# A hybrid encoder layer on one core: x's squares regrouped behind the projection of p, and the side work's steps with every twelve matmuls

## The chip, the cores and the metric

The kernel runs on one core of a Trainium2 chip. The metric is the device time of one execution in microseconds (us); lower is better. The engines are named as in the profile: PE is the matrix engine and PEld its weight loads, DVE the vector engine, ACT the scalar engine, POOL the general engine, and SP the engine whose queue issues nearly all DMAs here (SPq).

## The reference, cut to what matters

Two sequences (512 and 256 tokens) pass through one layer with the same weights. All 768 tokens are worked on together. Cut to what the change touches:

```
hn   = x * rsqrt(mean(x*x) + eps) * norm_g          # 768 x 2048
proj = hn @ w_in                                    # split into s_x, s_z, q, k, v, a_z, g_s, g_a
y    = s5(s_x, ssm parameters)                      # a state-space branch, two directions
...
h    = h + sigmoid(rmsnorm(h) @ ple_gate_w) * (p @ ple_proj_w)
```

`p @ ple_proj_w` doesn't depend on anything else, so the kernel does it first, while x is loaded. The sum of squares over the 2048 features gives one scale a token, and the kernel applies it to the results of the matmuls rather than to x.

## The kernel before, in words

x is held with features on the partitions: 16 tiles of 128 features by 768 tokens, loaded as eight pairs (`x_load`, 768 KB each, six buffers `xr`). Matmuls run on a high and a low half of each operand (ACT makes the high half, DVE the rest: `hh`/`hl` for x, in the trace tile `a`; `wh`/`wl` for weights), three products for each pair of halves.

The order of all work is written out by hand. `blocks` lists the matmul work; `run_blocks` walks it in groups of twelve matmuls. Around each group it calls `slot_e` (before) and `slot_p` (after). These let the side work go one step further: generators in a queue (`lane`), each of which has a part for ACT and DVE (E, before the group) and a part for PE (P, behind it). `pace[0]` is how far a group moves the step's counter: at 0.5 two groups share a step, at 0.7 ten groups have seven steps, at 1.0 each group has its own. `later(fn, n)` runs `fn` n steps on. Each engine works its instructions in the order of this program.

The stretch in question:

- Four `Proj` blocks, 16 groups, pace 0.5, so eight steps. Each group ends one 128 x 768 tile of `p @ ple_proj_w` in two banks of PSUM; ACT copies one half into a `stg` buffer, DVE the other (line 573), and a store (`d_pp`) follows one step later. There are five `stg` buffers and eight banks. With it runs the first part of the generator `x_gen`: step s makes the halves of x tiles 2s and 2s+1.
- Then eight s_x blocks (`Feat`), 64 groups, eight groups a block and four a weight piece. At the start of each piece `ahead` splits the piece after the next one (`wh`, `wl`, three buffers each). `x_gen` goes on: the rest of the squares (ACT, `sq`, three buffers) are added into `sqa` (DVE), two tiles a step; then `token_scale` sums `sqa` over partitions on PE (`ssps`), takes the root on POOL, and turns it into rows on PE (`rps`) for the tile `R`. No s_x result can leave PSUM before `R`; the first block's end is put off by five steps for that.
- Behind `x_gen` in the same queue stand the state-space steps: `s5_params` (bias matmuls `bb`, then small DVE operations on tiles `p_...`, and eight ACT copies into `tw` and `tq`), and then `s5_half(0)`, which waits until the fourth s_x block has left. Its first PE work is a transpose `wps` of DVE's product `w`. It sets its own pace (0.9, later 0.82 and 1.0).

After the regrouped part nothing else in the program is edited: `s5_half` starts by the block's end, not by the pace.

Of the kernel before, what the change touches and what calls it, by code (L numbers as in the profile page):

```python
# [28 lines left out]
class Lane:  # L29
# [5 lines left out]
    def add(self, gen):  # L35
        self.q.append(gen)
# [12 lines left out]
def build(tc, d, dbg=None):  # L49
    nc = tc.nc  # L50
    es = ExitStack()
    with es:
        es.enter_context(tc.manual_schedule())
        _build(tc, nc, d, es, dbg)


def _build(tc, nc, d, es, dbg):
# [20 lines left out]
    def act(out, in_, func=AF.Copy, **kw):  # L78
        return nc.scalar.activation(out=out, in_=in_, func=func, **kw)  # L79

    def tt(out, a, b, op):
        return nc.vector.tensor_tensor(out=out, in0=a, in1=b, op=op)  # L82
# [6 lines left out]
    def stt(out, a, s, b, op0, op1):  # L89
        return nc.vector.scalar_tensor_tensor(out=out, in0=a, scalar=s, in1=b, op0=op0, op1=op1)  # L90
# [7 lines left out]
    def dma(out, in_):  # L98
        return nc.sync.dma_start(out=out, in_=in_)  # L99
# [15 lines left out]
    pace = [0.5]  # L115
# [375 lines left out]
    def token_scale(acc, rs, rest=0):  # L491

        for _ in range(2 * rest):
            yield
        yield
        sp = bank(6, "ssps")
        for t in range(NT):
            mm(sp[:, 2 * t:2 * t + 2], acc[:, t * 128:(t + 1) * 128], ones[:, 0:2], True, True)
        yield
        rsqrt_mean(rs, sp[:, 0:2 * NT].rearrange("p (t x) -> p t x", x=2)[:, :, 0], D)  # L500
        rb = stg()
        for t in range(NT):
            ts(rb[:, t * 128:(t + 1) * 128], ones, rs[:, t:t + 1])
        yield
        rp = [bank(4, "rps"), bank(5, "rps")]
        for t in range(NT):
            nc.tensor.transpose(rp[t // 3][:, t % 3 * 128:t % 3 * 128 + 128], rb[:, t * 128:(t + 1) * 128], ident)
        yield
        act(R[:, :HT], rp[0][:, :HT])
        nc.vector.tensor_copy(out=R[:, HT:], in_=rp[1][:, :HT])  # L510
        yield
        yield
# [11 lines left out]
    def x_load(i):  # L524
        if i < 8:
            xraw[i] = ax.tile([128, 2, T], F32, tag="xr", name="xr", bufs=6)
            dma(xraw[i], d["xT"][:, 2 * i:2 * i + 2])

    def x_gen():

        sqs = []
        acc = ax.tile([128, T], F32, name="sqa")

        def square(k):
            sq = ax.tile([128, T], F32, tag="sq", name="sq", bufs=3)
            act(sq, xraw[k // 2][:, k % 2], AF.Square)
            sqs.append((k, sq))

        def add():
            while sqs:  # L540
                k, sq = sqs.pop(0)
                if k:
                    tt(acc, acc, sq, A_)
                else:
                    nc.vector.tensor_copy(out=acc, in_=sq)

        for s in range(8):
            add()
            for i in range(2):
                k = 2 * s + i  # L550
                x = xraw[s][:, i]
                act(hh[k], x, AF.Copy, scale=norm_g[:, k:k + 1])
                stt(hl[k], x, norm_g[:, k:k + 1], hh[k].bitcast(F32), M, S_)
            if 1 <= s < 5:
                square(s - 1)
            if s in (0, 3, 5):
                x_load({0: 5, 3: 6, 5: 7}[s])
            yield
            yield
        for s in range(4, 16, 2):  # L560
            add()
            square(s)
            square(s + 1)
            yield
            yield
        add()
        yield from token_scale(acc, rs_x)
        ax_es.close()
# [691 lines left out]
    def lam_gen():  # L1260

        pr = sm.tile([128, 2], F32, tag="lam", name="lampr")
        tt(pr, lamv[:, 0:2], lamv[:, 2:4], M)
        ts(subg8, subg, 0.8)
        yield
        lp = bank(7, "lamps")
        mm(lp[:, 0:2], ones, pr, True, True)
        yield
        e = sm.tile([128, 2], F32, tag="lam", name="lame")
        act(e, lp[:, 0:2], AF.Exp)  # L1270
        tt(nlam, e[:, 1:2], e[:, 0:1], S_)
        ts(nlam, nlam, -(0.8 - 0.6), None, A_)
        yield
        yield
# [604 lines left out]
    def run_blocks(lo, hi):  # L1879

        j = start_of[lo]
        while j < start_of[hi]:
            blk, pi = pieces[j]
            if isinstance(blk, Quad):
                run_quad(blk, j)
                j += 2
                continue
            if pi == 0:
                if blk.pre:
                    blk.pre()  # L1890
                blk.begin()
            ahead(j)
            wh, wl = halves.pop(j)
            for sub in range(4):
                prod[0] += 1
                hook(j, sub)
                run_events()
                if quad_of(j + 1):
                    for st in (("x",), ("a22",), ("s2",), ("y",))[sub]:
                        pieces[j + 1][0].step(st, j + 1)  # L1900
                    if sub == 3:
                        more()
                slot_e()
                blk.mms(pi, sub, wh, wl)
                slot_p()
            if blk in early:
                ahead(j + 1)
            if pi == len(blk.pieces) - 1:
                if blk.wait:
                    later(blk.end, blk.wait)  # L1910
                else:
                    blk.end()
                if blk.post:
                    blk.post()
            j += 1
# [52 lines left out]
    for i in range(2, 5):  # L1968
        x_load(i)
    wsplit(1)  # L1970
    lane.add(x_gen())
    lane.add(s5_all())
    run_blocks(0, end_p)
    j = start_of[first_k0]
    hooks[j, 0] = [lambda: lane2.add(t_prep(0))]
    lane.add(lam_gen())
    pace[0] = 0.7
    run_blocks(end_p, end_p + 4)
    run_blocks(end_p + 4, first_k0)
    while "s5" not in done:  # L1980
# [140 lines left out]
```

## Time and profile before

| what | value |
|---|---|
| median of three runs | 2394.75 us (2393.71 to 2396.52) |
| the profiled execution's own time | 2396.96 us |
| its span, first to last instruction | 2395.2 us |
| mean granted TensorE clock | 0.996 |

The span leaves out 1.8 us of the profiled execution's time. Busy times of the engines overlap each other. Idle time of an engine matters only where the engine that sets the end is the one idle.

### The profile page before, as it was taken

How to read it: one execution, taken by the hardware profiler on the slowest of the kernel's cores; microseconds unless marked ns; L12 is line 12 of the kernel's file. 1: busy time of each engine (PE TensorE's matmuls, PEld its weight loads, DVE VectorE, ACT ScalarE, POOL GpSimd, SP SyncE). 2: the span in 40 equal slices, each digit the busy share in tenths (PEclk: the TensorE clock that was granted, in tenths of full speed). 3: DMA queues.
4: the chain of work that ended last, by engine and by line, in shares of the span. 5: the costliest groups of instructions: out<-in, count | busy, mean ns of one | idle time of the engine just before them, and what ended most of it. 6: DMA issues, size and time to landing. Idle time of an engine off the chain costs nothing.

```text
span 2395.2 us, 36700 instructions
## 1 busy us (share of the span) xinstructions
PE 2352.4 (98%) x14278; PEld 2316.1 (97%) x14278; DVE 1442.2 (60%) x2689; ACT 1042.1 (44%) x1845; POOL 131.4 (5%) x158
## 2 busy tenths in 40 slices
PE   8999999999999999999999999999999999999997
PEld 8899999999999999999999999899999999999986
DVE  7577673566726677655667675556466655554346
ACT  7243214342135555554555555653233443533233
POOL 0000000000000000000121111000000011100000
PEclk9999999999999999999999999999999999999999
DMA  8344245432465677675867777456336485922235
GB/s 322 105 112 119 89 127 160 131 118 95 128 187 160 203 228 204 180 220 152 198 132 163 167 152 197 141 190 211 133 133 204 119 204 117 256 82 89 82 110 178
DMA packets 158157, 377.09 MB, mean 157 GB/s; under 512 B 34912, under 2 KB 57824, under 8 KB 157984
## 3 DMA queue, kind: packets, MB, share of 16 engines
q1 hardware_dynamic: 139264, 324.15, 41.4%
q0 software_dynamic: 18144, 49.55, 12.9%
q8 instruction: 112, 1.84, 0.3%
q10 hardware_dynamic: 576, 1.05, 0.1%
q14 instruction: 61, 0.50, 0.1%
HBM read 250.75 MB, written 129.43 MB: 159 GB/s over the span
## 4 chain that ended last, share of the span: by engine, by line
PE 86%; DMA 4%; DVE 4%; issue 3%; ACT 2%; SPq 1%; POOL 0%; POOLq 0%; ACTq 0%; DVEq 0%
PE acc L93 78%; PE yps L93 2%; PE o L93 1%; PE vps L93 1%; PE kps L93 1%; PE s L93 1%; DVE a L82 1%; DVE wl L82 1%; ACT wh L79 1%; DMA d_ga<-stg 1%; PE wps L1054 1%; SPq L99 1%; DMA xr<-in_xT 1%; DMA a<-in_xT 1%; ACT a L79 1%
## 5 line engine op out<-in xcount | busy, mean ns | idle before, releaser
L93 PE MATMUL acc<-a,wh 128*128 128x384 f32 (+2 forms) x5976 | 1331.1, 335 | 4.3 <-ACT stg L79 3.0
L93 PEld LDWEIGHTS acc<-a,wh 128*128 128x128 f32 x5976 | 1060.8, 188 | 12.7 <-ACT stg L79 3.9
L93 PE MATMUL acc<-a,wl 128*128 128x384 f32 (+2 forms) x3360 | 886.9, 337 | 6.6 <-DVE wl L82 3.7
L93 PEld LDWEIGHTS acc<-a,wl 128*128 128x128 f32 x3360 | 605.0, 188 | 16.5 <-DVE wl L82 4.1
L82 DVE TENSOR_TENSOR wl<-raw,wh 128x1024 fp32r<-128x1024 f32 (+1 forms) x280 | 340.7, 1217 | 425.5 <-ACT wh L79 420.3
L79 ACT ACTIVATE wh<-raw 128x1024 fp32r<-128x1024 f32 (+2 forms) x332 | 326.0, 983 | 297.3 <-PE acc L93 259.3
L79 ACT ACTIVATE stg<-acc 128x384 f32<-128x384 f32 x396 | 189.5, 489 | 382.1 <-PE acc L93 334.4
L93 PE MATMUL acc<-y,wh 128*128 128x384 f32 (+2 forms) x920 | 201.3, 335 | 0.0
L93 PEld LDWEIGHTS acc<-y,wh 128*128 128x128 f32 x920 | 162.7, 188 | 0.9
L93 PE MATMUL acc<-wh,a 128*128 128x256 f32 x768 | 138.8, 283 | 0.0
L79 ACT ACTIVATE stg<-stg 128x768 f32<-128x768 f32 (+3 forms) x64 | 43.3, 686 | 179.9 <-DVE stg L82 179.9
L93 PEld LDWEIGHTS acc<-wh,a 128*128 128x128 f32 x768 | 119.7, 192 | 0.0
L93 PE MATMUL acc<-y,wl 128*128 128x384 f32 (+2 forms) x400 | 109.8, 335 | 1.6 <-DVE wl L82 1.6
L93 PE MATMUL acc<-wl,a 128*128 128x256 f32 x384 | 109.8, 286 | 0.0
L93 PE MATMUL acc<-a,wa 128*128 128x384 f32 x504 | 94.8, 336 | 2.1 <-ACT stg L79 2.1
L93 PEld LDWEIGHTS acc<-a,wa 128*128 128x128 f32 x504 | 87.6, 188 | 2.9 <-ACT stg L79 2.8
L93 PEld LDWEIGHTS acc<-y,wl 128*128 128x128 f32 x400 | 72.9, 188 | 2.3 <-DVE wl L82 1.8
L82 DVE TENSOR_TENSOR raw<-raw,raw 128x512 f32<-128x512 f32 x104 | 71.9, 691 | 3.0
L93 PEld LDWEIGHTS acc<-wl,a 128*128 128x128 f32 x384 | 73.6, 192 | 0.0
L82 DVE TENSOR_TENSOR raw<-raw 128x512 f32<-128x512 f32 x104 | 71.6, 689 | 1.8
L82 DVE TENSOR_TENSOR stg<-stg,acc 128x384 f32<-128x384 f32 x52 | 28.8, 554 | 66.5 <-PE acc L93 52.6
L82 DVE TENSOR_TENSOR stg<-acc,R 128x384 f32<-128x384 f32 (+2 forms) x48 | 29.3, 656 | 63.4 <-PE acc L93 63.4
(251 smaller groups left out, 2319.0 us busy)
## 6 DMA issues: line engine op xcount, KB each, us to landing
raw<-in_w_in SPq DMA_DIRECT2D x144, 512.0 KB, 4.3
raw<-in_ple_g_w SPq DMA_DIRECT2D x42, 512.0 KB, 3.6
raw<-in_w_out SPq DMA_DIRECT2D x32, 512.0 KB, 4.1
d_h<-stg POOLq DMA_DIRECT2D x34, 384.0 KB, 6.6
d_gs<-stg POOLq DMA_DIRECT2D x28, 384.0 KB, 6.2
d_ga<-stg POOLq DMA_DIRECT2D x28, 384.0 KB, 5.9
d_q<-q SPq DMA_DIRECT2D x16, 512.0 KB, 3.7
raw<-in_w_v SPq DMA_DIRECT2D x16, 512.0 KB, 4.3
```

The lines of the kernel that those rows point to most:

```text
L79: return nc.scalar.activation(out=out, in_=in_, func=func, **kw)
L82: return nc.vector.tensor_tensor(out=out, in0=a, in1=b, op=op)
L93: return nc.tensor.matmul(out, lhsT, rhs, start=start, stop=stop, **kw)
L99: return nc.sync.dma_start(out=out, in_=in_)
L1054: nc.tensor.transpose(wps[x][:, g * 128:(g + 1) * 128], w[:, x, g], ident)
```

## The change

In the first eight steps, before: step s begins with the adds of the squares made earlier, then makes the halves of two tiles, and steps 1 to 4 make one square each (tiles 0 to 3). After: steps 1 and 3 make two squares each (tiles 0, 1 and 2, 3), behind the halves; steps 2 and 4 add them, two at a time, also behind the halves; the adds at the front of each step are gone. The loads of x pairs 6 and 7 go with steps 2 and 4 instead of 3 and 5. As many tiles as before (12) are squared in the s_x blocks. The pace in the s_x blocks until `s5_half` sets its own is 1.0 instead of 0.7.

```
-            add()
             for i in range(2):
                 ...
-            if 1 <= s < 5:
-                square(s - 1)
-            if s in (0, 3, 5):
-                x_load({0: 5, 3: 6, 5: 7}[s])
+            if s == 0:
+                x_load(5)
+            elif s in (1, 3):
+                for k in range(2):
+                    square(s - 1 + k)
+            elif s in (2, 4):
+                add()
+                x_load(s // 2 + 5)
             yield
             yield
...
     lane.add(lam_gen())
-    pace[0] = 0.7
+    pace[0] = 1.0
     run_blocks(end_p, end_p + 4)
```

## Rows read from the trace of the kernel before

**Rows 1.** The page: busy us of each engine, share of the span, instructions.

```profile
PE 2352.4 (98%) x14278; PEld 2316.1 (97%) x14278; DVE 1442.2 (60%) x2689; ACT 1042.1 (44%) x1845; POOL 131.4 (5%) x158
```

**Rows 2.** Waits of PE, first 160 us: us in total, times, longest.

```profile
PE wps L1054 <- DVE w L82: 3.0, 2, 1.6
...
PE ssps L93 <- DVE sqa L82: 0.2, 1, 0.2
```

**Rows 3.** Timeline of PE, 25 to 48 us: start, us, instruction [idle before].

```profile
34.81 0.33 PE L93 MATMUL acc<-ph,wh 128*128 128x384 f32 x1
36.10 0.44 PE L93 MATMUL acc<-ph,wh 128*128 128x384 f32 x1 [0.96 <-DVE stg L573]
...
44.41 0.51 PE L93 MATMUL acc<-a,wl 128*128 128x384 f32 x2
```

**Rows 4.** Timeline of ACT, from 29 us on.

```profile
29.64 1.00 ACT L79 ACTIVATE stg<-acc 128x384 f32<-128x384 f32 x2
30.54 1.05 ACT L79 ACTIVATE wh<-raw 128x1024 fp32r<-128x1024 f32 x1
...
44.07 1.77 ACT L79 ACTIVATE a<-xr,consts 128x768 fp32r<-128x768 f32 x2 [2.21 <-DMA xr<-in_xT]
...
47.76 3.12 ACT L79 ACTIVATE sq<-xr 128x768 f32<-128x768 f32 x4
...
126.82 2.28 ACT L79 ACTIVATE tw<-p_pw 64x512 f32<-64x512 f32 x2 [11.39 <-DVE p_pw L82]
...
135.91 1.06 ACT L79 ACTIVATE wh<-raw 128x1024 fp32r<-128x1024 f32 x1
```

**Rows 5.** Timeline of DVE, from 31 us on.

```profile
31.62 1.23 DVE L82 TENSOR_TENSOR wl<-raw,wh 128x1024 fp32r<-128x1024 f32 x1 [0.53 <-ACT wh L79]
32.77 0.95 DVE L82 TENSOR_TENSOR sqa<-sqa,sq 128x768 f32<-128x768 f32 x1
33.63 1.94 DVE L90 SCALAR_TENSOR_TENSOR a<-xr,consts,a 128x768 fp32r<-128x768 f32 x2
35.49 1.01 DVE L573 COPY stg<-acc 128x384 f32<-128x384 f32 x2
...
49.04 4.14 DVE L82 TENSOR_TENSOR sqa<-sqa,sq 128x768 f32<-128x768 f32 x4
54.02 1.23 DVE L82 TENSOR_TENSOR wl<-raw,wh 128x1024 fp32r<-128x1024 f32 x1 [0.84 <-ACT wh L79]
...
97.83 0.19 DVE L87 TENSOR_SCALAR p_xcp_dt<-p_ldt 128x64 f32<-128x64 f32 x1
...
127.67 0.19 DVE L861 COPY a8i<-p_pw 128x64 f32<-128x64 f32 x1
...
141.84 1.23 DVE L82 TENSOR_TENSOR wl<-raw,wh 128x1024 fp32r<-128x1024 f32 x1 [1.80 <-ACT wh L79]
...
146.36 0.69 DVE L82 TENSOR_TENSOR w<-t,t 128x512 f32<-128x512 f32 x1
```

**Rows 6.** Groups of DVE by line, 44 to 68 us: busy, mean ns, idle before.

```profile
L82 DVE TENSOR_TENSOR sqa<-sqa,sq 128x768 f32<-128x768 f32 x12 | 11.5, 957 | 0.8
```

**Rows 7.** DMA issues, 27.8 to 28.2 us: KB each, median us to landing.

```profile
xr<-in_xT SPq DMA_DIRECT2D x1, 768.0 KB, 7.8
```

**Rows 8.** The chain that ended last, first 160 us: start, us, what.

```profile
67.61 1.50 PE ssps L93 x12
...
72.48 8.34 PE acc L93 x48
```

**Rows 9.** Windows: stretch, length, busy of PE, PEld, DVE, ACT, POOL, PEclk, DMA.

```profile
140.00:150.00 10.00, 7.00 (x42) 6.45 (x42) 8.07 (x14) 2.63 (x4) 0.00 (x0) 1.00 0.33 120
```

**Rows 10.** Windows around the first fall of the clock, same columns.

```profile
409.00:412.00 3.00, 0.94 (x7) 0.81 (x7) 1.85 (x3) 1.06 (x1) 0.00 (x0) 0.94 0.98 268
412.00:415.00 3.00, 3.00 (x16) 3.00 (x16) 0.62 (x3) 0.00 (x0) 0.00 (x0) 0.50 0.59 176
```

**Rows 11.** Timeline of PE at that fall.

```profile
411.47 1.86 PE L93 MATMUL yps<-sb,q 128*128 128x96 f32 x8 [2.06 <-DVE wl L82]
```

## The prediction, as it was put on record before the run

> **What bounds the kernel now.** I read the page's busy times first: PE is busy 2352.4 of 2395.2 us [rows 1], so the whole idle time of PE is 43 us, and an edit off PE counts only by the PE idle it opens or closes. Next the waits of PE in the first 160 us, which is all that the edits reach: the reader sees 3.0 us in two waits of the transposes `wps` for DVE's `w` and 0.2 us of `ssps` for the sum of squares [rows 2]; the other waits there are the start and three short ones in the projection. Then the timelines of PE, ACT and DVE side by side. In the projection PE once waits 0.96 us for a DVE copy out of PSUM [rows 3]; from there to 142 us it runs without a gap, but for that 0.2. So the stretch holds little to win (about 3 us at 142 to 147 us, 1 us at 35), and DVE's order decides both. A group of twelve matmuls takes 8.34 / 4 = 2.085 us [rows 8].
>
> **The change part by part.**
>
> *What doesn't move.* I counted the pace's steps by hand. Before, the twelve late squares take groups 0 to 8 of the s_x blocks, `ssps` stands behind group 10, `R` at 12, the parameters' end at 33. After, the squares take groups 0 to 5, `ssps` stands behind group 6, `R` at 8, `tw`/`tq` at 20 (before 29), the parameters' end at 23. But `s5_half(0)` waits for the fourth block in both: its first step is at group 33 in both, its scan at 87, its output at 126, the end of the second half at 255. From group 126 on the two orders are almost the same. So no gain or loss is expected there; only the first 45 groups count. The 12 + 4 squares and adds are the same instructions.
>
> *Squares in the projection, two a step.* In step 3 ACT makes one more square ahead of the copies at 29.64 and of the weight half at 30.54 [rows 4]. A square in a row of four costs 3.12 / 4 = 0.78 us [rows 4]. So the weight half goes back by that, and DVE's `wl`, which waits for it, from 31.62 to 32.4 [rows 5]. On DVE the old order is `wl`, one add (0.86 to the next start), two x halves (1.86), then the copies at 35.49 [rows 5], the first of which lets PE go on at 36.10 [rows 3]. The new order is `wl` (1.15 to the next start), two halves (1.86), two adds, then the copies. Two adds into one `sqa` cost 1.06 + 0.86: four in a row take 4.14 with 0.957 for one [rows 5, 6], hence (4.14 - 0.96) / 3 = 1.06 from start to start. 32.4 + 1.15 + 1.86 + 1.92 = 37.3 for the copies, and PE went on 0.61 after their start (36.10 - 35.49), so now at 37.9: **+1.8 us**. Its gap there grows from 0.96 to between 2.4 and 2.8 us (its work before ends at 34.81 + 0.33, and comes some 0.3 later as its own copy waits for the extra square). Below, the bound is 0 (if the adds found room behind `wl`); above, 2.6 (no overlap at all). I take 1.8, all of its terms being rows.
>
> *The x loads.* Pair 6 is issued some 8 us sooner, ahead of two stores of p. A load issued at 27.87 landed 7.8 us later [rows 7]; ahead of the stores it can hold back theirs by up to 3 us, and with them the `stg` buffers four groups on. ACT reaches those after the landing, so I take 0; 1 us at the most. Pair 7 lands before its 2.21 us wait on ACT at 44.07 [rows 4]. That wait is off PE's path, but it lets ACT and DVE take up the 1.8 us: the first late square still starts near 47.6 (before 47.76 [rows 4]), the first add near 48.9 (before 49.04 [rows 5]), as PE begins s_x at 44.41 + 1.8 = 46.2 [rows 3].
>
> *Pace 1.0 in s_x: the sum of squares.* Twelve adds at 1.06 are 12.7 us, and one weight split (1.15) stands among them, with some 0.85 us of DVE idle before it, as before (0.84 at 54.02 [rows 5]). The ACT half queues behind a square that waits for a buffer, which an add must free. 48.9 + 14.7 = 63.6. PE comes to `ssps` after seven groups: 46.2 + 14.6 = 60.8. So PE now waits **2.85 us** for DVE, with all later s_x groups queued behind. Before, four more groups (8.3 us) covered this; this is the cover that the pace takes away. Less the old 0.2 us [rows 2]: with the projection, +4.5 us. If DVE starts an add or two sooner or later, this moves by 1 us either way.
>
> [...] With 0.957 for each the twelve adds would be 1.2 us shorter and the total that much lower.
>
> *The parameters, earlier.* On DVE they run from 97.83 to 127.86 [rows 5], and ACT copies `tw` and `tq` from 126.82 to 135.91 [rows 4]. They push back the weight half at 135.91, `wl`, then `wl` at 141.84 and `w` at 146.36 [rows 5], for which PE waits 3.0 us [rows 2]. After, PE comes to group 12 at 80.7 us (63.6, the 1.50 of `ssps` [rows 8], six groups, and about 3 us of other small matmuls). There DVE has a weight split and the first block's evacuation, some 3.8 us; from 84.5 the parameters follow without a gap. Between 97.83 and 127.86 they shared DVE with two splits and one evacuation, about 4 us, so they are 26 us; with two evacuations and two splits among them they end near 115, and the copies, 9.1 us, near 124. The split due at group 32 (126.3 us by the same count) stands behind the copies on ACT and comes at 126.4: it nearly fits. `w` is done near 144.9, its transposes are due at 145.1. I take **-2.7 us**, bounds 0 (if the `s5_half` loads come 3 us later) and -3.0.
>
> *The clock.* [...] At 140 to 150 us PE stood idle 3.0 us in all, in pieces of at most 1.6 [rows 2], and the clock stayed at 1.00 [rows 9]. The change opens gaps of about 2.4 and 2.85 us; each is longer than the gap with a fall. I take one fall; bounds none and two.
>
> *Sum.* +1.8 + 2.85 - 0.2 - 2.7 + 1.7 = **+3.5 us**. Against the profiled execution (2396.96 us, which is 2.2 above the median) that is 2400.5; against the median of the runs, 2394.75 + 3.5 = **2398.3 us**, +0.15%. A change of 0.2% is 4.8 us, about what a measurement of this kernel can tell from none.
>
> **The rivals.**
>
> *Slower: the clock falls behind both gaps.* Its place is 38 and 64 us. For it: both gaps are longer than the 2.06 us one. Against: only one gap of this size is in the rows I use, and the lengths are my working. It decides if what followed the gap at 409 us follows here twice. +1.8 (the sum without a fall) + 3.4 = +5.2 us, 2400.0; with the projection's 1 us for the stores, 2401. Chance 0.28.
>
> *The adds cost less, or DVE starts sooner.* With 0.957 us for an add, or without the 0.85 us in front of the split, the second gap is 1.7 to 2.0 us, and it may leave the clock alone. For it: a lone add lasts 0.957 [rows 6]. Against: the row of four at 4.14 [rows 5]. +1.8 - 1.2 = +0.6 up to +2.3 with one fall: 2395.4 to 2397. Chance 0.26. Here too belongs that the change does next to nothing on PE: if both its gaps and the old one at 142 us net out.
>
> *Faster: the old stall at 409 us goes with its fall.* The shift of the steps by a group in the half before it could bring the operand in time: -2.06 - 1.7 us, and -2.7 at 142 us, if the new gaps stay under 1 us. That is -5.5 us, 2389.3. Against: the steps stand at the same groups from 126 on, and the adds alone are 12.7 us for 14.6 us of groups, with a start 2.7 us late. Chance 0.06.
>
> **How the numbers follow.** The forecast with one fall has 0.40, and gives 2397.3 to 2399.4 by the bounds of its terms. Faster 0.06 (the last rival), slower 0.28 (the first), same 0.66. The range runs from the cheaper adds, 2395.4, less 1 us for DVE's start and 1 us for the spread of the runs, 2393.5, to both falls, 2400, with 2.5 us for the stores and for the split that nearly fits, 2402.5; outside lie most of the last rival and the tail of the others.
>
> **What the profile after would show.** PE waits for `ssps` some 2.85 us near 61 to 64 us (below 1 us: the add chain is wrong). The wait for the copy near 35 to 38 us is over 2 us (unchanged: the order on DVE was misread). The granted clock shows a new piece at the lower level near 38 or 64 us. The `wps` wait near 145 us is under 0.5 us; `tw` and `tq` are done by 125 us. From 150 us on everything is the old trace, moved by one amount. The prediction fails if a wait appears that I did not find, above all PE at group 32 for its weight split, which has 0.1 us to spare by my working, or if the later stalls move.

## The result, and the profile after

The changed kernel takes 2412.38 us (median of four runs, 2408.68 to 2414.26) against 2395.64 us for the kernel before, run beside it: ratio 1.0063, 95% interval 1.0048 to 1.0077. The forecast was 2398.3 us, +0.15%, and the range ended at 2402.5: wrong, by some 14 us. The profiled execution took 2412.77 us, its span is 2411.0 us.

The page first, busy times (answers to [rows 1]). PE's busy time grows by 6 us of the 16; the rest is idle time of PE.

```profile
span 2411.0 us, 36698 instructions
PE 2358.6 (98%) x14278; PEld 2323.9 (96%) x14278; DVE 1444.0 (60%) x2689; ACT 1040.6 (43%) x1845; POOL 130.8 (5%) x158
```

**The first 160 us.** The waits of PE (answers to [rows 2]; us in total, times, longest) and PE's timeline (start, us, instruction, [idle before]; answers to [rows 3, 8]):

```profile
PE ssps L93 <- DVE sqa L82: 2.4, 1, 2.4
PE acc L93 <- DVE stg L577: 2.2, 1, 2.2
```

```profile
34.77 0.34 PE L93 MATMUL acc<-ph,wh 128*128 128x384 f32 x1
37.28 0.44 PE L93 MATMUL acc<-ph,wh 128*128 128x384 f32 x1 [2.17 <-DVE stg L577]
...
47.15 0.51 PE L93 MATMUL acc<-a,wl 128*128 128x384 f32 x2
...
64.30 2.14 PE L93 MATMUL ssps<-ones,sqa 128*128 128x2 f32 x12 [2.43 <-DVE sqa L82]
...
148.92 1.03 PE L1058 MATMUL wps<-consts,w 128*128 128x128 f32 x8
```

Both gaps that the prediction announced are there: 2.17 us for the copy out of PSUM (before 0.96) and 2.43 us for the sum of squares (before 0.2). The transposes `wps` run in one piece, without a wait. DVE's timeline shows why (answers to [rows 5, 6]):

```profile
31.81 1.23 DVE L82 TENSOR_TENSOR wl<-raw,wh 128x1024 fp32r<-128x1024 f32 x1 [1.12 <-ACT wh L79]
...
34.81 1.95 DVE L82 TENSOR_TENSOR sqa<-sqa,sq 128x768 f32<-128x768 f32 x2
36.68 1.01 DVE L577 COPY stg<-acc 128x384 f32<-128x384 f32 x2
...
49.84 6.27 DVE L82 TENSOR_TENSOR sqa<-sqa,sq 128x768 f32<-128x768 f32 x6
...
58.05 6.20 DVE L82 TENSOR_TENSOR sqa<-sqa,sq 128x768 f32<-128x768 f32 x6
...
138.32 0.23 DVE L82 TENSOR_TENSOR u<-kr,bc 128x64 f32<-128x64 f32 x1 [4.73 <-DMA bc<-in_bc]
...
145.91 0.69 DVE L82 TENSOR_TENSOR w<-t,t 128x512 f32<-128x512 f32 x1
```

The copy starts at 36.68 behind the two adds; the twelve adds end at 64.25 (58.05 + 6.20). The second `w` starts at 145.91, almost as before (146.36 [rows 5]). PE doesn't wait for it because PE itself is late. The windows show the clock (length, then busy of PE, PEld, DVE, ACT, POOL, then PEclk and DMA; answers to [rows 9, 10]):

```profile
36.00:40.00 4.00, 2.72 (x9) 2.72 (x10) 4.00 (x7) 3.30 (x5) 0.00 (x0) 0.71 0.90 353
...
65.00:68.00 3.00, 3.00 (x13) 3.00 (x13) 0.16 (x1) 0.00 (x0) 1.21 (x1) 0.50 0.00 0
...
140.00:150.00 10.00, 10.00 (x63) 9.96 (x62) 8.21 (x13) 2.40 (x3) 0.00 (x0) 1.00 0.30 99
409.00:412.00 3.00, 3.00 (x24) 3.00 (x24) 0.00 (x0) 1.51 (x4) 0.00 (x0) 1.00 0.39 77
412.00:415.00 3.00, 3.00 (x20) 3.00 (x19) 0.00 (x0) 0.88 (x4) 0.00 (x0) 1.00 0.86 249
```

The clock falls to 0.50 behind both gaps (in each us from 38 to 41, with 0.71 in the mean of 36 to 40; and in each from 65 to 71), and the stall near 411 us with its fall [rows 10, 11] isn't there.

**Where the 16 us are.** PE does the same 12,624 matmuls into `acc` in the same order in every kernel here. So I set each against the same one of the kernel before. The table gives how many us later it starts, at times of the kernel before, worked out from the traces of one profiled execution each. How far two executions scatter is seen from the line of e11: on every engine it runs the same instructions in the same order as the kernel before, and the two lie up to 3.6 us apart. So a difference of 2 or 3 us between two lines shows nothing by itself. (e1 to e12 are the experiments below.)

```
us            44   125   165   405   418  1250  1320  1470  1600  2380
after        2.7   7.7   3.8   5.9   2.0   4.0  12.7  19.2  15.8  16.0
e1           3.4   6.7   2.8   6.3   2.4   4.5   7.2   6.8   6.4   6.4
e2          -0.3  -0.3  -0.3  -0.3  -4.2  -1.7   6.9  13.3  10.2  10.3
e8           0.2   0.2   0.2   0.2  -3.7  -0.5   7.5   9.1   6.3   6.2
e11          0.1   0.1   2.5   2.5  -1.4   1.4   2.6   2.5   3.6   2.9
e3           1.6   1.6   2.7   2.7   0.0   1.5   2.3   4.1   4.5   4.7
e4           0.0   6.5   2.6   4.6   0.7   1.3   1.0   1.1   2.6   1.8
e7           1.4   6.4   6.4   8.1   6.8   4.5   4.2   4.4   5.1   5.2
e5           1.1   4.4   0.5   4.0   0.1   2.8   4.8   9.3   5.8   6.0
e6           0.0   0.1   2.4   2.4  -1.2   0.0  -1.0  -0.7   0.4  -0.1
e9           0.1   5.6   1.7   5.2   1.3   2.2   2.6   2.6   2.7   2.9
e10         -0.4   5.0   1.2   4.7   2.5   2.3   2.2   2.4   1.8   1.9
e12         -0.3  -0.2  -0.2  -0.2  -3.6  -3.0  -1.7  -3.1  -0.4  -0.9
```

The first line answers the question of place: at 165 us the changed kernel is 3.8 us late, close to the forecast of 3.5. Then it stays between 2 and 6 us late until 1250 us. From there to 1600 us it loses another 11.8 us: in the attention, more than a millisecond behind the last edited line. The waits of PE in that stretch, 1060 to 1600 us of each kernel, before and after:

```profile
PE acc L93 <- ACT stg L79: 5.1, 5, 1.6
...
PE wt L1387 <- DVE p L90: 4.1, 1, 4.1
```

```profile
PE acc L93 <- ACT stg L79: 14.5, 8, 4.8
PE s L93 <- ACT ot L79: 3.1, 3, 1.2
```

The wait for ACT's copy out of PSUM goes from 5.1 to 14.5 us, and one for `ot` is new. The longest, 4.83 us, is followed through three engines in the changed kernel's timelines of DVE, ACT and PE:

```profile
1280.57 1.82 DVE L82 TENSOR_TENSOR kl<-raw,kh 128x768 fp32r<-128x768 f32 x2
...
1285.61 0.69 DVE L82 TENSOR_TENSOR wh<-raw,wh 128x512 fp32r<-128x512 f32 x1 [0.27 <-ACT wh L79]
1288.38 0.96 DVE L90 SCALAR_TENSOR_TENSOR raw<-raw,R 128x768 f32<-128x768 f32 x1 [2.07 <-DMA raw<-d_qq]
1291.43 0.96 DVE L90 SCALAR_TENSOR_TENSOR raw<-raw,R 128x768 f32<-128x768 f32 x1 [2.09 <-DMA raw<-d_qq]
1292.31 0.69 DVE L82 TENSOR_TENSOR raw<-raw 128x512 f32<-128x512 f32 x1
```

```profile
1293.09 0.63 ACT L79 ACTIVATE wl<-raw 128x512 fp32r<-128x512 f32 x1 [5.94 <-DVE raw L82]
1293.62 1.56 ACT L79 ACTIVATE qh<-raw 128x768 fp32r<-128x768 f32 x2
1295.09 0.47 ACT L79 ACTIVATE stg<-acc 128x384 f32<-128x384 f32 x1
```

```profile
1295.61 2.61 PE L93 MATMUL acc<-a,wh 128*128 128x384 f32 x7 [4.83 <-ACT stg L79]
```

Read it from the bottom. PE needs a PSUM bank that ACT empties at 1295.09. Ahead of that copy ACT has a weight's half `wl`, which waits 5.94 us for DVE's `raw` at 1292.31. Ahead of that DVE has the scaling of q, which waits twice for the reload of q from `d_qq`. That reload goes into the buffer that k has just left (`kl`, done at 1282.39), so it is issued then, from 1282.45 us on, and DVE starts on its halves 5.9 and 9.0 us later. Before, the scaling of q costs a 1.32 us wait on DVE, 2.64 on ACT and 0.68 on PE. It also stands at another place in DVE's order: ahead of the weight's `wh`, where the changed kernel has it behind (1285.61 above). DVE's rows of the kernel before, then PE's:

```profile
1280.72 1.87 DVE L90 SCALAR_TENSOR_TENSOR raw<-raw,R 128x768 f32<-128x768 f32 x2 [1.32 <-DMA raw<-d_qq]
1282.50 0.68 DVE L82 TENSOR_TENSOR wh<-raw,wh 128x512 fp32r<-128x512 f32 x1
```

```profile
1284.94 2.35 PE L93 MATMUL acc<-a,wh 128*128 128x384 f32 x12 [0.68 <-ACT stg L79]
```

What put the steps of the attention elsewhere? A counter: `slot_p` adds the pace behind each group and closes the step when the sum reaches 1 (the next `slot_e` opens a new one); what is left over stays. After the state-space steps both kernels stand at group 256, as I had counted, but the rest left in the counter (`open_[1]`) is 0.16 before and 0.56 after. By the count of the program the two part where the state-space steps set their own pace: 35 groups at 0.7 leave a rest of 0.50, 34 at 1.0 leave none, and the stages behind carry this on.

The paces that follow group 256 are the same in both, so the rest lives on. At pace 0.5 (715 to 993 us in the kernel before) two groups share a step, and it depends on the rest, below or above a half, which two. The attention enters the queue at 993 us: with 0.16 in the middle of an open step, with 0.56 at the start of one. By the count of the program this, with 24 groups at 0.9, puts its parts half a step later, so that they change places with what the program writes between two groups: halves of weights and copies out of PSUM. Where the loss arises, from 1250 us on, the pace is 1.0 (until 1506 us) and each group has its own step in both kernels; what differs there is the order on DVE and ACT.

### The profile page after: what moved, and what is told of

Its sections match the earlier page's. It is cut to its first block, busy times and chain, and to the rows that moved or that the text cites. A ratio compares the mean times of both kernels' runs of the same rounds, so it can differ in the third digit from the quotient of the medians.

```text
span 2411.0 us, 36698 instructions
## 1 busy us (share of the span) xinstructions
PE 2358.6 (98%) x14278; PEld 2323.9 (96%) x14278; DVE 1444.0 (60%) x2689; ACT 1040.6 (43%) x1845; POOL 130.8 (5%) x158
## 4 chain that ended last, share of the span: by engine, by line
PE 85%; DMA 5%; DVE 4%; ACT 3%; issue 2%; SPq 1%; POOL 0%; POOLq 0%; ACTq 0%; DVEq 0%
PE acc L93 78%; PE yps L93 1%; PE vps L93 1%; PE kps L93 1%; PE o L93 1%; SPq L99 1%; PE s L93 1%; DVE a L82 1%; ACT wh L79 1%; ACT a L79 1%; DMA raw<-d_qq 1%; DMA d_o<-ot 1%; ACT stg L79 1%; PE wps L1058 1%; DMA stg<-d_y 1%
```

## The experiments

All ratios are against the kernel before, run beside each on the same chip, with 95% intervals. My theory: the counter's rest makes the loss in the attention. The rival: some resource state, a queue or a lateness that the change carries along, makes it.

**The counter alone, both ways.** e1 is the changed kernel with the old rest; e2 is the kernel before with the new rest, and nothing of the change.

```
     while "s5" not in done:
         slot_e()
         slot_p()
+    open_[1] = 0.1599999999999877      # e1; in e2 0.5599999999999894
```

e1: 

> The changed kernel, but where the state-space steps are done (group 256) the fraction left in the pace's counter is set to 0.16, which is what the kernel before has there; the changed one has 0.56. Nothing else differs. Theory of the counter: from group 256 on each step falls on the same group as before again, so the loss in the attention (lag 5.9 us at 1084 us, 18 at 1450) goes, and only the first 150 us cost: the lag there was 3 to 4 us, so 2396 + 3.5 = 2399 us, 2397 to 2402. Rival, the shift: the attention loses because it runs 4 us later against its transfers, or by some other state carried on; then this stays near 2412.

Measured: 1.0014 (1.0005 to 1.0024), 2400.91 us.

e2: 

> The kernel before with the counter set to 0.56 at group 256, nothing else changed. Theory of the counter: the whole loss of the attention appears without any part of the change, 2396 + 12 = 2408 us (2405 to 2412), with the two long waits near 1290 and 1385 us. Rival, the shift: nothing moves before group 256, so 2396 us.

Measured: 1.0045 (1.0029 to 1.0060), 2409.07 us. The table has the same in its stretches: from 1250 to 1600 us e1 loses 1.9 us, e2 11.9, the changed kernel 11.8. And e2's rows of DVE and PE repeat those of the changed kernel:

```profile
1282.18 0.96 DVE L90 SCALAR_TENSOR_TENSOR raw<-raw,R 128x768 f32<-128x768 f32 x1 [2.11 <-DMA raw<-d_qq]
1285.30 0.96 DVE L90 SCALAR_TENSOR_TENSOR raw<-raw,R 128x768 f32<-128x768 f32 x1 [2.16 <-DMA raw<-d_qq]
```

```profile
1289.48 4.21 PE L93 MATMUL acc<-a,wh 128*128 128x384 f32 x12 [4.93 <-ACT stg L79]
```

So the loss there is the counter's, shown from both sides. The rival falls: e1 comes 4.5 us late to the attention and loses little, e2 comes 1.7 us early and loses all.

**Other rests.** The kernel before with 0.86 (e8) and 0.36 (e11) in the same line.

e8: 

> The kernel before with the counter at 0.86 at group 256. Theory of the counter says that the phase matters, not which way it goes: I expect a loss of a few us, 2396 to 2408, or none, and the waits of the attention at other places than with 0.16 or 0.56. Rival (the loss comes from 0.56 being later than 0.16 by two fifths of a step, so more of it costs more): 2412 us or more.

Measured: 1.0039 (1.0025 to 1.0052). The loss is of the size that I expected, but not by waits at other places: PE's long wait near 1285 us is that of e2 (4.97 us, in e2 4.93), and the second one, near 1385 us, is missing in this execution.

e11: 

> The kernel before with the counter's rest set to 0.36 instead of 0.16 at the end of the state-space steps, halfway to the 0.56 that the change leaves. My theory (what counts is which group of the seven products the reload of q and its scaling fall in, a step function of the rest): either nothing (1.000) or most of the loss (1.003 to 1.005), and the waits for the ACT copy at 1283 to 1296 us show which. Rival (the loss grows evenly with the rest): about half of 0.56's, 1.002.

Measured: 1.0006 (0.9997 to 1.0015). The traces show why. Every engine of e11 runs the instructions of the kernel before in the same order, from the first to the last; and e8 has e2's order but for one place near 1070 us on DVE and on ACT. So the four rests give two orders, not four: 0.16 and 0.36 the one, 0.56 and 0.86 the other. By the runs' medians the first order costs nothing (1.0006) and the second 0.4% (1.0045 and 1.0039, with intervals that overlap). That is the step function which I expected, with the outcome "nothing" for 0.36; the even growth of the rival (1.002) lies outside the interval.

In the profiled execution of e11 DVE waits 3.29 us for q and PE 1.88 us, where the kernel before has 1.32 and 0.68:

```profile
1283.40 1.83 DVE L90 SCALAR_TENSOR_TENSOR raw<-raw,R 128x768 f32<-128x768 f32 x2 [3.29 <-DMA raw<-d_qq]
```

```profile
1287.58 2.35 PE L93 MATMUL acc<-a,wh 128*128 128x384 f32 x12 [1.88 <-ACT stg L79]
```

As the order is the same, this is scatter: the two loads of q landed 8.0 us after their issue in e11 and 5.9 us in the kernel before (medians). So are the 2.2 us that e11 loses between 1250 and 1600 us in the table, and no more can be read from the 11.9 of e2 and the 6.8 of e8, which have one order there.

**The reload of q taken away.** In e5 (changed kernel) and e6 (kernel before) q isn't loaded again; both go on with k's tile in its place, so their outputs are not the layer's, and they serve for the time alone.

```
-            rw = atile("raw", (128, 2, T), F32)
-            for c in range(2):
-                dma(rw[:, c], src[...])
+            if n == "k":
+                rw = atile("raw", (128, 2, T), F32)
+                for c in range(2):
+                    dma(rw[:, c], src[...])
```

e5: 

> The changed kernel (counter 0.56) without the reload of q's tiles in the attention's preparation: it goes on with k's tile in place of q, so the attention's scores are others; all steps, engine instructions and matmuls stay, and eight loads of 384 KB fall out. Theory of the load: with the counter at 0.56 the load is issued about 4 us (three groups less the split in front of it) ahead of its use, lands 8 us after its issue, and DVE, with all weight splits and copies queued behind, holds PE for 4 to 5 us twice and drops the clock. Without it the attention's loss goes: 2412 - 11 = 2401 us, the same as with the counter put back (ratio 1.0014). Rival, the other waits of the phase (the single buffer of the output tile, PE's scores behind it): 2408 us or more.

Measured: 1.0024 (1.0015 to 1.0034), 2402.17 us.

e6: 

> The same edit (no reload of q's tiles, k's in their place) in the kernel before, as the control: what the loads cost where they come in time. Theory of the load: 2396 us less at most 2, as DVE waits 3.3 us there and PE hardly; rival: if the loads as such (3 MB on the queues) cost, it falls as far as the changed kernel does.

Measured: 0.9992 (0.9983 to 1.0001), 2393.88 us. Without the reload the two kernels differ by 8.3 us instead of 16.7, and the changed kernel's loss between 1250 and 1600 us is 3.0 instead of 11.8 us. So two thirds to three quarters of it go through the wait for q (8.4 of some 12 to 13 us by the medians, 8.8 of 11.8 by the traces). The rest stays with e5: its waits of PE there still have the new one for `ot`.

```profile
PE acc L93 <- ACT stg L79: 7.7, 5, 3.3
PE s L93 <- ACT ot L79: 3.1, 3, 1.2
```

A buffer of its own for q, which would let its reload start earlier, wasn't tried.

**The parts of the change.** e3 has the regrouped squares with pace 0.7, e4 the old squares with pace 1.0, e7 the old squares with pace 0.8; e4 and e7 with the rest set to 0.16.

```
-    pace[0] = 1.0
+    pace[0] = 0.7       # e3; in e7, with the old squares, 0.8
```

e3: 

> Only the regrouped squares, adds and x loads, with the pace of before (0.7), so the counter at group 256 is 0.16 as before. Theory of the counter: only the projection's longer wait, 1.2 us by the trace of the changed kernel (2.17 us in place of 0.96), and a fall of the clock behind it (1.7 us): 2397 to 2399.5 us, no loss in the attention. Rival, the squares carry it: with their part of the shift, 2405 us or more.

Measured: 1.0008 (0.9998 to 1.0019), 2398.92 us.

e4: 

> Only the pace (1.0 in place of 0.7), with the squares of before, and the counter at group 256 set to 0.16 as before. My sum for the first 150 us has the sum of squares ready by the chain of twelve adds, whatever the projection loses: PE then waits some 4.5 us for it in place of 2.4, the clock falls once behind it (1.7 us), and 2 to 3 us come back at 145 us: 2396 + 3.5 = 2399 us, 2397.5 to 2401. If the two gaps add up rather than cover each other, 2397.5 or less. Rival, the shift: 2405 us or more.

Measured: 1.0011 (1.0002 to 1.0021), 2400.23 us. Alone, pace 1.0 makes PE wait 3.93 us for the sum of squares:

```profile
63.09 2.30 PE L93 MATMUL ssps<-ones,sqa 128*128 128x2 f32 x12 [3.93 <-DVE sqa L82]
```

In the changed kernel it is 2.43, as PE comes 2.7 us later from the projection. The regrouped squares' delay is thus partly the cover for the pace's wait; the two costs don't add up.

e7: 

> The squares of before, the pace 0.8 in place of 0.7 (or 1.0), and the counter put at 0.16 at group 256. By my account of the first 150 us the chain of adds is done 17.4 us into the s_x blocks; at 0.8 the sum of squares stands behind group 8, 18.8 us in, so PE doesn't wait for it, and the parameters' copies go at group 25 rather than 29, some 8 us sooner, so the 3.0 us at 145 us go as well: 2396 - 3 = 2393 us, ratio 0.9987 (0.998 to 1.000). Rival, any pace above 0.7 loses the cover of the sum: 1.000 to 1.002.

Measured: 1.0020 (1.0012 to 1.0029): a miss. PE still waits for the sum at pace 0.8:

```profile
67.12 1.95 PE L93 MATMUL ssps<-ones,sqa 128*128 128x2 f32 x12 [2.38 <-DVE sqa L82]
```

The sum stands two groups later than in e4, but a weight half made at group 8 now stands ahead of the last two adds on DVE (its row starts at 63.98, theirs at 65.12 with 1.94 us). The 3.0 us at `wps` stay as well, though PE comes to them late: `bc` is late too, and the second `w` starts at 150.65.

```profile
143.06 0.23 DVE L82 TENSOR_TENSOR u<-kr,bc 128x64 f32<-128x64 f32 x1 [5.05 <-DMA bc<-in_bc]
```

**The first 160 us: can they gain?** e9 and e10 have the old squares, pace 1.0, rest 0.16, and the sum put off by three more steps; e9 and e12 issue the load of `bc` ahead of the stores of s_x (e12 at pace 0.7 and without the later sum).

```
-        yield from token_scale(acc, rs_x)
+        yield from token_scale(acc, rs_x, 3)        # e9, e10
...
         load_bc(0)
         load_bc(1)
+        while f"sx{hf}" not in done:                # e9, e12: moved here
+            yield
+            yield
+        load_u(0)
```

e9: 

> The old order of the squares with pace 1.0 in the s_x blocks, the sum of squares put off by three more steps (it stands behind group 9 instead of 6), the counter's rest at 0.16 at the end of the state-space steps, and the load of the bias row (bc) issued ahead of the eight stores of s_x instead of behind them. My theory (the wait of the transposes wps for DVE's w comes from that load): no wait for the sum of squares over 0.5 us, no wps wait, the attention as before; some 3 us less than before, 2392 to 2393, ratio 0.9987. Rival (the wps wait comes from the parameters and their copies being late, or the load isn't what ends it): the wait stays at about 3 us, ratio 1.000.

Measured: 1.0017 (1.0008 to 1.0026).

e10: 

> The same without the earlier bc load. My theory: no wait for the sum of squares, but the wps wait stays near 3 us although tw and tq are ready some 10 us earlier, as DVE then waits for the bc load: ratio 1.000 (0.9995 to 1.0005). Rival (tw and tq were the cause, as my prediction had it): the wps wait goes here too, ratio 0.9987.

Measured: 1.0012 (1.0004 to 1.0021).

e12: 

> The kernel before (old squares, pace 0.7), with the bc load alone moved ahead of the stores of s_x; the counter's rest 0.16 as before. My theory by now (the bc load and the late tw and tq copies both end near 138 us, either alone is enough): the wps wait shrinks by 1 us at most, ratio 1.000. Rival (the load alone is the cause): the wait goes, ratio 0.9987.

Measured: 0.9999 (0.9990 to 1.0008), the `wps` wait unchanged. The edit tests little: it brings the issue of the load forward by 0.7 us only (133.62 to 132.94), and DVE waits for `bc` in neither.

```profile
PE wps L1057 <- DVE w L82: 3.0, 2, 1.6
```

The waits for the sum and at `wps` are gone in e9 and e10, but a new one has come at group 32, the same in both (e10 is shown):

```profile
125.89 0.70 PE L93 MATMUL acc<-a,wl 128*128 128x384 f32 x2 [4.05 <-DVE wl L82]
```

That is the weak spot which the prediction named: the weight half behind the copies `tw` and `tq` on ACT. A PE that arrives without the earlier gaps arrives too early for it. The clock falls behind this gap as well (0.53 from 126 to 129 us in e10). So the wait only changed its place here. My expectation for e9, a version ahead of the kernel before, was wrong, and so was the one for e10, in which the `wps` wait should have stayed. No kernel of these is faster than before beyond the interval.

## Why the prediction was wrong

**The step that failed** is in *What doesn't move*: "From group 126 on the two orders are almost the same. So no gain or loss is expected there; only the first 45 groups count." I had compared the groups at which the stages begin, and those are the same. I had not carried the rest of the counter, 0.16 against 0.56, into the paces that follow. The attention loses 11.8 of the 16 us; with the old rest the same code loses 1.9 there (e1), so some 10 us are the rest's, and e2 has them without any of the change (11.9 us by the medians). The sentence that would have caught it stood in the last part, "if the later stalls move", but with no chance and no price.

**The first 160 us were right in the total:** +3.8 us at 165 us, forecast +3.5; and e1, the change without the counter's effect, measured 1.0014 against a forecast of 1.0015. That they agree so well is luck in part: the falls of the clock cost 2.5 us more than forecast, the two gaps 1.0 us less, and the parameters gave back 1.2 us more. By its terms:

- *The projection.* Forecast +1.8, the gap alone measured 2.17 - 0.96 = 1.2. The copies started at 36.68, I had 37.3: the extra square put `wl` back by 0.2 (31.62 to 31.81), not by 0.78, as ACT got its `stg` buffer 0.4 us sooner (26.46 against 26.86) and its two copies took 0.86 against 1.00.
- *The x loads.* Taken as 0, and no cost shows: PE's two waits for ACT's copies of before (1.25 and 0.40 us, at 27 and 30 us) are even gone. The up to 3 us by which pair 6 might hold back the stores was an estimate, and no run shows it: ACT's waits for a `stg` buffer behind `d_pp`, from 20 to 48 us, come to 4.1 us, before to 6.7.
- *The sum of squares.* Forecast 2.85 less 0.2, measured 2.43 less 0.2. The adds go at (6.27 - 0.96) / 5 = 1.06 us from start to start, as read from [rows 5], while one lasts 958 ns in the mean (951 to 961 over all fifteen). So the 0.957 us of [rows 6] is the duration of one, not their distance. PE came at 61.9 (I had 60.8), the adds ended at 64.25 (63.6).
- *The clock.* Forecast one fall, 1.7 us; there were two. The 1.7 is what the two windows of [rows 10] lose, 3 x 0.06 + 3 x 0.50 us, around the 2.06 us gap of [rows 11] in that one execution of the kernel before. With s_x 2.74 us late (44.41 to 47.15), the first cost 2.74 - 1.21 = 1.5 us; between 44 and 125 us the kernel loses 7.7 - 2.7 = 5.0, of which 2.2 are the gap, so the second cost about 2.7 us. This was the slower rival's mechanism, with 0.28; its total of +5.2 was too high by the two smaller gaps and by the next point.
- *The parameters.* Forecast -2.7; the table gives 3.8 - 7.7 = -3.9 between 125 and 165 us. The size is near, the cause is not the one I gave. `tw` and `tq` were done at 124.3 us as forecast, but then DVE waits 4.73 us for `bc`, and `w` comes only 0.4 us sooner. The wait is gone because PE comes late and `w` doesn't: the delays ahead of it are given back in part. Lateness alone isn't enough, as e7 shows, where `bc` and `w` are late too. In the kernel before the late copies end at 135.91, and the two loads of `bc`, issued from 133.62 on, land 2.6 us after their issue (median), so at about the same time. That either alone would hold `w` fits these rows; no run here takes both away with PE on time.
- *The split at group 32*, "0.1 us to spare": PE didn't wait there in the changed kernel, and waited 4.05 us in e9 and in e10, where it came sooner.

**The other rivals.** "From 150 us on everything is the old trace, moved by one amount" is refuted by the table. The cheaper adds of the second rival were not there: they go at 1.06 us. The faster rival leaned on the stall at 411 us [rows 11]; but e2, e6, e8 and e11 do the same work as the kernel before up to 600 us and don't show the stall (they gain 3.6 to 3.9 us between 405 and 418 us). It was an event of that one execution, not of the program, and nothing could be won by it.

## What to carry to other kernels

When a schedule is driven by a running sum, an edit changes not only the steps inside its stretch but the remainder that it hands on: carry the remainder through every later stage, or set it anew at a stage's border, before calling the rest of the trace unmoved. Where two versions are to be compared, list each engine's instructions in order: where the lists are equal, a difference in time is scatter (here up to 3.6 us, e11). A wait that disappears behind a new delay is not a gain; ask whether its producer came sooner or its consumer later. And a stall that stands in one execution's trace is no term of a forecast until a second execution of the same code shows it.

## What the runs showed of the hardware

The same wait brought a fall of the clock in one execution and none in another. e1 and e3 have the same work up to 44 us, and in both PE waits 2.09 us for the copy out of PSUM at 37.6 to 38 us. The windows behind it, e1 and then e3:

```profile
39.00:42.00 3.00, 3.00 (x12) 3.00 (x11) 3.00 (x5) 1.65 (x3) 0.00 (x0) 0.53 1.03 341
```

```profile
39.00:42.00 3.00, 3.00 (x19) 3.00 (x18) 3.00 (x5) 1.37 (x3) 0.00 (x0) 1.00 1.01 309
```

In e1 the clock is at 0.53 (12 matmuls in 3 us), in e3 at 1.00 (19). I had treated a fall as a thing that a gap of a given length brings or doesn't. By these two runs it is better taken as a chance, at 1.5 to 2.7 us a fall (the two falls of the changed kernel, as worked out above).

The prediction leaned on this in one more place: it took from [rows 9] that PE's 3.0 us of idle time at `wps` leave the clock alone. The same order in e11, with the same two waits (1.63 and 1.40 us), shows a fall there. The kernel before and then e11:

```profile
146.00:149.00 3.00, 1.89 (x13) 1.90 (x14) 2.97 (x5) 0.00 (x0) 0.00 (x0) 1.00 0.03 11
```

```profile
146.00:149.00 3.00, 1.74 (x7) 1.74 (x8) 2.96 (x5) 0.00 (x0) 0.00 (x0) 0.58 0.05 19
```

e6 and e2, with the same work up to there, have 0.57 and 1.00 in this window.
